# Turns as products on diagonal tiles, and key products that alternate between two row halves

## The chip, the cores and the metric

The kernel runs on one core of one Trainium2 chip. A core has TensorE (PE: matrix products, with a sequencer for loading weights, PEld), VectorE (DVE), ScalarE (ACT), GpSimd (POOL) and a queue for transfers (SP). The metric is the device time of one execution, in microseconds (us); lower is better. A time is the median of several runs.

## The reference, cut to what matters

A decoder trunk of four layers over 512 tokens of width 1024, in float32. Every layer is a mixer followed by a gated MLP with a short convolution. The mixers are sparse attention, mLSTM, the delta-rule mixer (RWKV-7), and sparse attention again. The change is in the delta-rule mixer, of which there is one. It has 16 heads of width 64:

```python
def step(state, inp):
    r_t, w_t, k_t, v_t, kk_t, a_t = inp
    removed = jnp.einsum('bhij,bhj->bhi', state, kk_t)
    state = (state * w_t[:, :, None, :] - removed[..., None] * (kk_t * a_t)[:, :, None, :]
             + v_t[..., None] * k_t[:, :, None, :])
    return state, jnp.einsum('bhij,bhj->bhi', state, r_t)

_, y = lax.scan(step, jnp.zeros((B, H, N, N), f32), (tm(r), tm(decay), tm(k), tm(v), tm(kk), tm(a)))
...
y = ((y - mean) * lax.rsqrt(var + RWKV_GN_EPS)).reshape(B, T, D) * ln_w + ln_b
```

Projections come before this recurrence, a group norm, a gate and an output projection behind it.

## The kernel before, in words

The whole trunk is one program. Features lie on the 128 partitions, tokens along the row, so the mixer holds its 16 heads as 8 pairs: the first head of a pair on partitions 0 to 63 (`hv[0]`), the second on 64 to 127 (`hv[1]`). The 512 tokens are 8 chunks of 64.

The recurrence is computed by chunks. For each pair of heads six stages run one after the other: `prep` (decays and scaled operands), `inverse` (products within a chunk, the keys turned, the first levels of a triangular inverse), `last` (the other levels, and `inverted`), two halves of `scan` (the state from chunk to chunk), and `output` (group norm, gate). A loop of 13 steps starts a new pair at each step, so up to six pairs are under way, each at another stage.

Two helpers matter here.

`turn` transposes a 64x64 block of one head by means of PE and the identity. A block that ends on the lower partitions is a transpose instruction (L1664), one that ends on the upper partitions a product with the identity (L1666). It is called for both heads of a pair one after the other: 4 times in `inverse`, 4 times in `inverted`, and twice 8 times in `output` (once for the values that `scan` left, tile `sv`, and once for the normed output, tile `tmp`). That is 24 turns of both heads for each pair of heads. A turn's weights and operand lie on one head's 64 partitions, its result on 64 partitions of PSUM, so it uses one quarter of the PE array. For the values the result lies on the other head's partitions, so these two quarters are the ones off the diagonal.

The key products (L1761) multiply 64 rows of `KB` (keys of both kinds, 128 columns) with two blocks of `LW`. They use 64 rows and all columns of the array: the row half of their head. For each pair of heads there are 16, four for each head and half of the chunks, and each four fill one PSUM bank (`iv`), which three VectorE instructions then read.

Other small products of the loop: L1752 (64x64 products of both heads on the two diagonal tiles), L1775 (keys transposed, 128x128), L1804, L1812, L1819 (levels of the inverse), L1847, L1849, L1861, L1868 (the scan), L1876 (its output).

The order on every engine isn't the order in which the code is written. `Order` takes the traced program, gives each instruction a cost and each dependency a latency, makes list schedules forwards and backwards in turn for each phase, and keeps the best; the whole mixer is one phase. For PE it knows three things that matter here: a transpose counts 2 passes and an f32 product 4; the clock is taken to be half if too few columns went through the array in the tick before (`TICK`, `WARM`); and a product whose output is at most 64 rows and lies on the upper half is taken to run beside the one before it, if that was on the lower half and less than `BESIDE` ago (fields `alone`, and `lower` in `run`).

Of the kernel before, what the change touches and what calls it, by code (L numbers as in the profile page):

```python
# [26 lines left out]
# the FFN's blocks by Winograd's seven products instead of eight, and where its down projection goes on to the next chunks  # L27
# [4 lines left out]
def interleave(live):  # L32
    """advance generators [gen, done, expected] so that they finish together"""
    live = list(live)
    while live:
        it = min(live, key=lambda v: v[1] / v[2])
        try:
            next(it[0])
            it[1] += 1
        except StopIteration:  # L40
            live.remove(it)
# [11 lines left out]
BESIDE = 22  # L53

class Order:
    """a static order for every engine: list schedules of the traced program, forwards and backwards in turn"""

    def __init__(self, traced):
        ins = [i for i in traced if type(i).__name__.startswith("Inst")]  # L60
        self.ins, n = ins, len(ins)
        self.pred = [dict() for _ in ins]      # name -> latency after the end
        self.follow = [set() for _ in ins]     # starts after the start of
        self.eng, self.dur, self.table, self.rows, self.load, self.alone = [], [], [], [], [], []
# [9 lines left out]
        for k, i in enumerate(ins):  # L74
# [5 lines left out]
            # columns through the whole of the array  # L80
            self.rows.append(math.prod(x[1] for x in list(i.outs[0].bass_ap.ap)) * list(i.ins[0].bass_ap.ap)[0][1]
                             * self.passes(i) / 16384 if e == "PE" else 0)
            # weights load beside the product before, if that is long enough;
            # a product on the upper half of the array runs beside the one before on the lower
            self.load.append(0.0)
            self.alone.append(None)
            if e == "PE":
                p, rows = self.box(i.outs[0])[7:]
                wide = i.ins[0].dtype in (mybir.dt.float32, F32R) and not i.is_transpose
                self.load[k] = rows * (1 + wide) / 2.4  # L90
                if rows <= 64:
                    self.alone[k] = self.dur[k] if p else 0
                    if p:
                        self.dur[k] = BESIDE
# [23 lines left out]
        # a slot is free again when the tile whose users end first has been used  # L118
# [15 lines left out]
        # the memory of a pool is free for the next when all its users are through  # L134
# [10 lines left out]
        # phases: each opens its pools when those of the one before are closed  # L145
# [37 lines left out]
    def box(a):  # L183
        """(tile, in PSUM, partitions, columns, tile object); a PSUM bank is held whole, by readers too"""
# [62 lines left out]
    def run(self, prio, back=False, origin=0.0):  # L247
# [11 lines left out]
        table, short, lower = None, 0, False  # L259
        ticks = collections.defaultdict(float)  # columns that left the array  # L260
        for _ in range(n):
# [19 lines left out]
            if e == "PE" and not back:  # L281
# [5 lines left out]
                if self.alone[k] and not (lower and t - free[e] < BESIDE):  # L287
                    d += self.alone[k] - dur[k]
                    short = self.alone[k]
                else:  # L290
                    short = dur[k]
                lower = self.alone[k] == 0
# [26 lines left out]
    def part(self, a, b):  # L319
        """the instructions from a to b by themselves"""  # L320
        p = object.__new__(Order)
        for name in ("ins", "eng", "dur", "table", "rows", "load", "alone"):
            setattr(p, name, getattr(self, name)[a:b])
# [6 lines left out]
    def turns(self, prio, rounds, origin=0.0):  # L330
        """the best of the schedules forwards and backwards in turn"""
# [10 lines left out]
    def best(self, tries=24, rounds=10, keep=4, log=None):  # L342
        """phase by phase: schedules of the phase by itself, the best of them tried behind the phases before"""
# [34 lines left out]
class Core:  # L378
# [33 lines left out]
    def spill(self, i, src):  # L412
        """the residual leaves the chip"""
# [11 lines left out]
    def psum(self, **banks):  # L425
        """shares the banks out to the uses of a phase"""
# [20 lines left out]
    def weights(self, ap, pool=False, raw=None, parts=None, pieces=1):  # L447
        """a unit's high and low parts"""
# [83 lines left out]
    def combos(self, g, ap):  # L532
        """Winograd's sums of the quarters of h (chunks k | k + 4, token halves): [B11 - B12 | B22 + that],
        [B12 - B22 | B21 - the second], in two parts each"""
# [26 lines left out]
    def ffn(self, ly, gcur, gnext, nsplit=True):  # L561
        nc, tc, A = self.nc, self.tc, self.A
        H = T // 2
        with ExitStack() as es:
# [15 lines left out]
            def gate(b, G):  # L580
                """convolution and silu"""
# [28 lines left out]
            def mm(ps, w, k0, rhs, start, stop):  # L610
                """four chunks of a quarter product"""
# [7 lines left out]
            def seven(b):  # L619
                """gate and value of block b by Winograd's seven products: rows (gate, value), chunk halves, token halves"""  # L620
# [58 lines left out]
            def down_part(p, o):  # L679
                """a part's share of output o, with the shares of the parts before"""  # L680
# [61 lines left out]
    def fm_steps(self, units, xhi, xlo, out, m=128, tag="ps", every=2, pool=False):  # L742
        """fm_block in pieces; appends the bank to out"""
# [13 lines left out]
    def stack_block(self, unit, xhi, xlo, m, dst, room, tag="ps"):  # L757
        """narrow product: both weight parts side by side, two passes; dst = sum of the halves"""
# [19 lines left out]
    def nsa(self, j, gnext):  # L778
        nc, tc, A = self.nc, self.tc, self.A
        te, ve, ac, po = nc.tensor, nc.vector, nc.scalar, nc.gpsimd  # L780
        with ExitStack() as es:
# [16 lines left out]
            # token-major values, high and low parts side by side  # L798
# [97 lines left out]
            with ExitStack() as cs:  # L896
# [36 lines left out]
                # gates  # L933
# [4 lines left out]
                # compression  # L938
                raws = [fp.tile([128, 1024], F32, name="cw1", tag="cw1", bufs=3) for _ in range(8)]
                for i in range(2):  # L940
# [7 lines left out]
                    for k in range(16):  # L948
                        if (i, k) == (1, 0):
                            next(val)  # L950
                        if k % 4 == 0:
                            # the values' place is still free
# [42 lines left out]
            def cmp_soft(g):  # L995
# [23 lines left out]
                # block-diagonal compressed values of this group  # L1019
# [27 lines left out]
            def first_block():  # L1047
                # of the output, as far as the heads are through
# [9 lines left out]
            def scores(i):  # L1058
# [4 lines left out]
                for qbs in ((0, 1), (2,), (3,)):  # L1063
                    bank = self.ps(tag="s")
                    pss = []
                    # the masks of the diagonal blocks first, and what follows is added
# [116 lines left out]
    def mlstm(self, j, gnext):  # L1183
# [3 lines left out]
        with ExitStack() as es:  # L1187
# [30 lines left out]
            # gates  # L1218
# [182 lines left out]
            # per-head scale, tokens on partitions  # L1401
# [33 lines left out]
    def rwkv(self, j, gcur, gnext):  # L1435
# [4 lines left out]
        with ExitStack() as es:  # L1440
# [6 lines left out]
            # halves for the tanh forms of the sigmoids  # L1447
# [31 lines left out]
            # room that the second half of the values takes later  # L1479
# [6 lines left out]
            # the residual leaves the chip for this part, its place is taken by the normed input  # L1486
# [8 lines left out]
            def narrow(unit, n):  # L1495
                # the step from the token before follows the product, with weights scaled for it beside the plain ones
# [27 lines left out]
            for i in range(DC):  # L1524
                po.memset(Hn[i][:, 7:8], 0.0)
                ve.scalar_tensor_tensor(Hn[i][:, 8:], self.x[i], gcur[:, i:i + 1], self.R, op0=OP.mult, op1=OP.mult)
                # the step from the token before, kept where the values come later
# [33 lines left out]
            # kept where the groups' operands come later  # L1561
# [14 lines left out]
            # normaliser of the removal keys  # L1576
# [37 lines left out]
            def values(c):  # L1614
                # tokens of a chunk on the half that the other head's state leaves free
# [37 lines left out]
            def block_diagonal(p):  # L1653
                # operands that are zero beside their blocks
# [5 lines left out]
            def turn(out, src, e, low):  # L1660
                # a transpose that ends on the upper partitions is a product with the identity
                eye = self.ident[hv[e], hv[e]]
                if low:
                    te.transpose(out, src, eye)  # L1664
                else:
                    te.matmul(out, src, eye, start=True, stop=True)  # L1666
# [9 lines left out]
            def prep(p):  # L1676
# [38 lines left out]
                # bonus coefficients on every feature of the head  # L1715
# [7 lines left out]
                # scaled operands; first head of the pair holds (-b|k), second (k|-b)  # L1723
# [16 lines left out]
            def inverse(p):  # L1740
                g = G[p]
                KB, LW = g["KB"], g["LW"]
                # in-chunk products
# [11 lines left out]
                for e in range(2):  # L1755
                    kr, br = hv[1 - e], hv[e]
                    for q in range(2):
                        ps = self.ps((128, 4, 2, 64), tag="iv")
                        for i in range(4):
                            c = 4 * q + i  # L1760
                            te.matmul(ps[:, i], KB[br, c], LW[br, e:e + 2, c], start=True, stop=True)  # L1761
                        cs4 = slice(4 * q, 4 * q + 4)
# [6 lines left out]
                # keys with tokens on partitions  # L1769
# [411 lines left out]
```

## Time and profile before

| | us |
|---|---|
| three runs | 3009.51, 3031.78, 3043.8 |
| their median | 3031.78 |
| profiled execution, span of the core | 3045.1 |
| mean granted PE clock in it | 0.943 |

The profiled execution is one execution besides the three; its span, from the first to the last instruction, is the time that the rows of the trace add up to, and it lies 13 us above the median of the runs. In the views, PE rows with f32 products count two records for each product. Matmuls are pipelined, so durations of neighbours overlap: what a run of products costs is read from its start to the start of what comes next. The granted clock is given as a share of full speed.

### The profile page before, as it was taken

Reading aid. Unit: us, or ns where it says so; the run is one execution under the profiler, and the core shown is the slowest. Engines: PE = TensorE matmul, PEld = TensorE weight load, DVE = VectorE, ACT = ScalarE, POOL = GpSimd, SP = SyncE. Lnnn points to the kernel's source line nnn. Section 1 sums busy time; section 2 is a strip of 40 time slices with the busy share of each in tenths; the row PEclk is TensorE's granted clock in tenths of the full one; section 3 lists DMA queues with packets and bytes.
Section 4 is the critical chain, followed back from the end, with each engine's and each line's share of the span. In section 5 each row is a group of like instructions: output and inputs, shape, how many; then the busy total and the mean of one; then the engine's idle time right before and its main releaser. Section 6 shows DMA issues by size and latency. Waiting matters only on the chain. (4 is left out here: it accounts for less than half of the span.)

```text
span 3045.1 us, 48538 instructions
## 1 busy us (share of the span) xinstructions
PE 2936.2 (96%) x17768; PEld 2450.8 (80%) x17768; DVE 2357.0 (77%) x4225; ACT 1622.7 (53%) x3290; POOL 814.5 (27%) x898
## 2 busy tenths in 40 slices
PE   7999999999999999989899999999999999999998
PEld 6777899997777999867666666689997777889996
DVE  8688789988788898886565533499987788888995
ACT  4677655544665554435454433355543677755543
POOL 5476300001351000034664332200003467400001
PEclk8999999999999999999986656899999999999999
DMA  4100223454123334532100000223445210133344
GB/s 159 59 29 22 91 98 122 135 158 142 65 88 121 105 122 143 163 122 84 42 5 4 5 19 30 92 96 121 135 153 161 77 37 27 39 125 110 131 135 149
DMA packets 115422, 283.28 MB, mean 93 GB/s; under 512 B 14448, under 2 KB 26224, under 8 KB 115184
## 3 DMA queue, kind: packets, MB, share of 16 engines
q1 hardware_dynamic: 115184, 280.18, 28.0%
q8 instruction: 140, 2.29, 0.3%
q14 instruction: 98, 0.80, 0.1%
HBM read 248.67 MB, written 31.46 MB: 92 GB/s over the span
## 5 line engine op out<-in xcount | busy, mean ns | idle before, releaser
L461 ACT ACTIVATE whi<-wraw 128x1024 fp32r<-128x1024 f32 (+2 forms) x344 | 272.3, 792 | 453.9 <-PE ps L469 292.0
L616 PE MATMUL ps<-h,shi 128*128 128x256 f32 x1728 | 353.7, 281 | 0.0
L462 DVE TENSOR_TENSOR wlo<-wraw,whi 128x512 fp32r<-128x512 f32 (+2 forms) x306 | 275.8, 902 | 81.8 <-ACT whi L461 78.7
L616 PE MATMUL ps<-bhi,slo 128*128 128x256 f32 x1152 | 322.9, 281 | 0.1
L616 PE MATMUL ps<-blo,shi 128*128 128x256 f32 x1152 | 321.9, 281 | 0.0
L616 PE MATMUL ps<-bhi,shi 128*128 128x256 f32 x1152 | 321.9, 281 | 0.0
L601 POOL MEMSET tmp<- 128x2 f32 x88 | 8.3, 100 | 1097.9 <-DVE tmp L594 873.8
L616 PEld LDWEIGHTS ps<-h,shi 128*128 128x128 f32 x1728 | 282.8, 188 | 7.4
L469 PE MATMUL ps<-alo,whi 128*128 128x512 f32 x704 | 278.3, 396 | 0.0
L468 PE MATMUL ps<-ahi,wlo 128*128 128x512 f32 x704 | 277.0, 394 | 0.0
L467 PE MATMUL ps<-ahi,whi 128*128 128x512 f32 x704 | 276.8, 395 | 0.0
L467 PE MATMUL ps<-h,whi 128*128 128x512 f32 x672 | 265.2, 399 | 4.8 <-ACT whi L461 1.4
L468 PE MATMUL ps<-h,wlo 128*128 128x512 f32 x672 | 263.8, 394 | 1.8 <-DVE wlo L462 1.5
L469 PE MATMUL ps<-h,whi 128*128 128x512 f32 x672 | 263.7, 394 | 0.0
L616 PE MATMUL ps<-h,slo 128*128 128x256 f32 x864 | 242.6, 281 | 0.0
L734 DVE TENSOR_TENSOR slo<-sum,shi 128x512 fp32r<-128x512 f32 x288 | 197.3, 686 | 44.8 <-ACT shi L733 43.0
L733 ACT ACTIVATE shi<-sum 128x512 fp32r<-128x512 f32 x288 | 179.4, 624 | 94.6 <-DVE sum L636 67.1
L616 PEld LDWEIGHTS ps<-bhi,slo 128*128 128x128 f32 x1152 | 217.0, 188 | 5.5 <-DVE slo L734 0.5
L616 PEld LDWEIGHTS ps<-bhi,shi 128*128 128x128 f32 x1152 | 216.5, 188 | 4.3 <-ACT shi L733 0.2
L616 PEld LDWEIGHTS ps<-blo,shi 128*128 128x128 f32 x1152 | 216.5, 188 | 1.5
L501 POOL TENSOR_TENSOR tmp<-tmp 128x512 f32<-128x512 f32 x62 | 97.1, 1566 | 351.8 <-ACT tmp L496 347.3
L1089 POOL TENSOR_SCALAR P<-P,st,GT 128x128 f32<-128x128 f32 (+3 forms) x256 | 161.5, 646 | 86.3 <-DVE st L1087 53.6
(677 smaller groups left out, 7977.1 us busy)
## 6 DMA issues: line engine op xcount, KB each, us to landing
wraw<-in_fup_dram SPq DMA_DIRECT2D x104, 512.0 KB, 3.6
fraw<-in_fup_dram SPq DMA_DIRECT2D x72, 512.0 KB, 3.5
wraw<-in_fdn_dram SPq DMA_DIRECT2D x128, 256.0 KB, 2.8
share<-xt SPq DMA_DIRECT2D x64, 256.0 KB, 2.1
xt<-share SPq DMA_DIRECT2D x64, 256.0 KB, 3.0
wraw<-in_fdn_dram SPq DMA_DIRECT2D x64, 192.0 KB, 2.5
x<-spill SPq DMA_DIRECT2D x48, 256.0 KB, 3.1
spill<-x SPq DMA_DIRECT2D x47, 256.0 KB, 2.6
```

Source lines behind the costliest of these rows:

```text
L461: nc.scalar.activation(hi[:, s], raw[:, s], AF.Copy)
L462: (nc.gpsimd if pool else nc.vector).tensor_tensor(lo[:, s], raw[:, s], hi[:, s].bitcast(F32), op=OP.subtract)
L467: t.matmul(ps, whi, xhi, start=start, stop=False)
L468: t.matmul(ps, wlo, xhi, start=False, stop=False)
L469: t.matmul(ps, whi, xlo, start=False, stop=stop)
L501: nc.gpsimd.tensor_tensor(a2, self.acc[0], sq, op=OP.add)
L601: nc.gpsimd.memset(G[:, 0:2], 0.0)
L616: nc.tensor.matmul(ps, lhs[:, s], x, start=start and k + i == 0, stop=k == 3 and i == 2, skip_group_check=True)
L733: self.nc.scalar.activation(hi, src, AF.Copy)
L734: self.nc.vector.tensor_tensor(lo, src if src2 is None else src2, hi.bitcast(F32), op=OP.subtract)
L1089: po.tensor_scalar(P[qb], P[qb], st[:, 2, qb:qb + 1], GT[:, qb, 3 * h + 1 + br:3 * h + 2 + br], op0=OP.mult, op1=OP.mult)
```

## The change

It has three parts, all for the delta-rule mixer's small products.

1. `turn` always makes a product with the identity, for both heads. The transposes on the lower half (L1664) are gone; the line is L1670 now.
2. In `inverse`, the key products of one half of the chunks are written for both heads in turn, into two banks, chunk by chunk (L1765); before, all those of the first head came first, then those of the second. What reads the banks is unchanged but for its order.
3. `Order` now also takes a product that uses 64 rows and more than 64 columns of the array to run beside the one before it, if that was of the same kind and on the lower row half. A new field `side` tells the kinds apart: 1 for products with at most 64 output rows, as before, 2 for those with at most 64 operand rows.

Comments are removed as well. No tile, size or transfer is changed.

```diff
@@ Order.__init__
             if e == "PE":
                 p, rows = self.box(i.outs[0])[7:]
+                kind = 1
+                if rows > 64:
+                    b = self.box(i.ins[0])
+                    p, kind = b[2], 2
+                    if b[3] - b[2] > 64:
+                        kind = 0
                 wide = i.ins[0].dtype in (mybir.dt.float32, F32R) and not i.is_transpose
                 self.load[k] = rows * (1 + wide) / 2.4
-                if rows <= 64:
+                if kind:
+                    self.side[k] = kind
                     self.alone[k] = self.dur[k] if p else 0
                     if p:
                         self.dur[k] = BESIDE
@@ Order.run
-                if self.alone[k] and not (lower and t - free[e] < BESIDE):
+                if self.alone[k] and not (lower == self.side[k] and t - free[e] < BESIDE):
                     d += self.alone[k] - dur[k]
                     short = self.alone[k]
                 else:
                     short = dur[k]
-                lower = self.alone[k] == 0
+                lower = self.side[k] if self.alone[k] == 0 else 0
@@ Core.rwkv
-            def turn(out, src, e, low):
-                eye = self.ident[hv[e], hv[e]]
-                if low:
-                    te.transpose(out, src, eye)
-                else:
-                    te.matmul(out, src, eye, start=True, stop=True)
+            def turn(out, src, e):
+                te.matmul(out, src, self.ident[hv[e], hv[e]], start=True, stop=True)
...
-                for e in range(2):
-                    kr, br = hv[1 - e], hv[e]
-                    for q in range(2):
-                        ps = self.ps((128, 4, 2, 64), tag="iv")
-                        for i in range(4):
-                            c = 4 * q + i
-                            te.matmul(ps[:, i], KB[br, c], LW[br, e:e + 2, c], start=True, stop=True)
-                        cs4 = slice(4 * q, 4 * q + 4)
+                for q in range(2):
+                    pss = [self.ps((128, 4, 2, 64), tag="iv") for _ in range(2)]
+                    for i in range(4):
+                        c = 4 * q + i
+                        for e in range(2):
+                            te.matmul(pss[e][:, i], KB[hv[e], c], LW[hv[e], e:e + 2, c], start=True, stop=True)
+                    cs4 = slice(4 * q, 4 * q + 4)
+                    for e in range(2):
+                        kr, br = hv[1 - e], hv[e]
+                        ps = pss[e]
                         ve.tensor_tensor(MT[br, 2 * q:2 * q + 2], ps[br, 0::2, e],
                                          m_su[br, None, :].to_broadcast([64, 2, 64]), op=OP.mult)
...
-                        turn(pg[hv[e], d], F2[hv[e], d], e, e == 0)
+                        turn(pg[hv[e], d], F2[hv[e], d], e)
```

The other three calls of `turn` lose their last argument in the same way.

More of the change, by code (lines that the diff above doesn't have):

```diff
@@ L63, in __init__ @@
         self.follow = [set() for _ in ins]
-        self.eng, self.dur, self.table, self.rows, self.load, self.alone = [], [], [], [], [], []
+        self.eng, self.dur, self.table, self.rows, self.load, self.alone, self.side = [], [], [], [], [], [], []
         tiles, users, tags = {}, collections.defaultdict(list), collections.defaultdict(list)
@@ L86, in __init__ @@
             self.alone.append(None)
+            self.side.append(0)
             if e == "PE":
                 p, rows = self.box(i.outs[0])[7:]
+                kind = 1
[4 more added lines that the diff above has]
+                        kind = 0
                 wide = i.ins[0].dtype in (mybir.dt.float32, F32R) and not i.is_transpose
                 self.load[k] = rows * (1 + wide) / 2.4
-                if rows <= 64:
+                if kind:
+                    self.side[k] = kind
                     self.alone[k] = self.dur[k] if p else 0
@@ L258, in run @@
                 heapq.heappush(wait[eng[k]], (0.0, prio[k], k))
-        table, short, lower = None, 0, False
+        table, short, lower = None, 0, 0
         ticks = collections.defaultdict(float)
@@ L321, in part @@
         p = object.__new__(Order)
-        for name in ("ins", "eng", "dur", "table", "rows", "load", "alone"):
+        for name in ("ins", "eng", "dur", "table", "rows", "load", "alone", "side"):
             setattr(p, name, getattr(self, name)[a:b])
@@ L1830, in inverted @@
                     for e in range(2):
-                        turn(pg[hv[e], d], F[hv[e], d], e, e == 0)
+                        turn(pg[hv[e], d], F[hv[e], d], e)
                 g["XT"] = XT = pair(rk())
@@ L1901, in output @@
                     for e in range(2):
-                        turn(pt[hv[e], c], S[hv[1 - e], c, e, :], 1 - e, e == 0)
+                        turn(pt[hv[e], c], S[hv[1 - e], c, e, :], 1 - e)
                 ve.tensor_tensor(c8(bon), pt, c8(bon), op=OP.mult)
@@ L1907, in output @@
                     for e in range(2):
-                        turn(pt[hv[e], c], c8(yc)[hv[e], c], e, e == 0)
+                        turn(pt[hv[e], c], c8(yc)[hv[e], c], e)
                 ac.activation(yf, pt.rearrange("p c t -> p (c t)"), AF.Identity, scale=vec(LNW, p), bias=vec(LNB, p))
```

## The prediction

> **What bounds the kernel now.** I read the page's first two parts, then busy time by stretches, then PE's rows in order of time inside the delta-rule mixer.
>
> From the page: engines, then PE and its granted clock in 40 slices of 76 us.
>
> ```profile
> PE 2936.2 (96%) x17768; PEld 2450.8 (80%) x17768; DVE 2357.0 (77%) x4225; ACT 1622.7 (53%) x3290; POOL 814.5 (27%) x898
> ...
> PE   7999999999999999989899999999999999999998
> ...
> PEclk8999999999999999999986656899999999999999
> ```
>
> PE is busy nearly everywhere, and its clock is full but for slices 21 to 26: the mixer's loop over pairs of heads, which I take as 1500 to 1960 us.
>
> The view by stretches (us, then busy time of PE, PEld, DVE, ACT, POOL, granted clock, DMA):
>
> ```profile
> 1500.00:1684.00 184.00, 177.87 (x1395) 126.73 (x1393) 114.66 (x257) 95.61 (x278) 101.81 (x122) 0.80 0.02 4
> 1684.00:1960.00 276.00, 275.60 (x1799) 185.60 (x1796) 106.61 (x286) 99.53 (x320) 81.91 (x89) 0.65 0.09 28
> 1960.00:3045.10 1085.10, 1049.79 (x6467) 920.43 (x6465) 905.63 (x1643) 603.28 (x1169) 231.35 (x272) 0.99 0.33 108
> 1684.61:1688.02 3.41, 3.41 (x31) 2.35 (x30) 1.18 (x3) 0.68 (x4) 3.41 (x5) 1.00 0.00 0
> 1688.02:1691.43 3.41, 3.41 (x23) 2.48 (x22) 1.79 (x5) 1.51 (x6) 0.05 (x1) 0.50 0.09 24
> 1740.00:1760.00 20.00, 20.00 (x112) 12.16 (x112) 5.90 (x13) 5.63 (x18) 4.68 (x6) 0.50 0.01 4
> ```
>
> In the loop PE idles 6 of 460 us, while DVE, the next engine, is busy 221. The clock is 1.00 or 0.50, never between, in steps of 3.41 us; from 0.80 and 0.65 follows 184 x 0.40 + 276 x 0.70 = 267 us at half clock. So the loop costs what PE's products cost at the clock they get, and what PE saves is saved.
>
> **The turns.** PE in order of time: start, duration, operation. Durations overlap, so I go from start to start. First half clock, then full, then runs of L1752, which has what a turn has after the change: 64x64 products of both heads on two diagonal tiles, into one bank. A product in f32 is two records.
>
> ```profile
> 1640.53 0.31 PE L1664 MATMUL a<-ident,sv 64*64 64x64 f32 x1
> 1640.77 0.47 PE L1666 MATMUL a<-ident,sv 64*64 64x64 f32 x2
> 1641.17 0.31 PE L1664 MATMUL a<-ident,sv 64*64 64x64 f32 x1
> ...
> 1571.01 0.24 PE L1664 MATMUL iv<-ident,h 64*64 64x64 f32 x1
> 1571.18 0.33 PE L1666 MATMUL iv<-ident,h 64*64 64x64 f32 x2
> 1571.44 0.24 PE L1664 MATMUL iv<-ident,h 64*64 64x64 f32 x1
> ...
> 1586.99 0.68 PE L1752 MATMUL iv<-wraw,LW 64*64 64x64 f32 x16
> 1587.60 0.33 PE L1868 MATMUL sa<-sv,wlo 128*64 128x64 f32 x2
> ...
> 1776.89 1.11 PE L1752 MATMUL iv<-wraw,LW 64*64 64x64 f32 x14
> 1777.93 0.58 PE L1761 MATMUL iv<-LW,wraw 64*128 64x128 f32 x1
> ```
>
> A pair of turns (transpose for one head, product for the other) takes 0.64 us at half clock and 0.43 at full. Diagonal products take 0.61 us for four pairs at full clock, 0.15 a pair; 1.04 for three and a half at half clock, 0.30 a pair; entering and leaving the run is in it.
>
> ```profile
> L1664 PE MATMUL a<-ident,sv x64: 242/310/313, 1638.0 to 1943.0; 64*64 64x64 f32 x64
> L1664 PE MATMUL a<-ident,tmp x64: 241/309/314, 1646.8 to 1956.7; 64*64 64x64 f32 x64
> L1664 PE MATMUL iv<-ident,h x56: 213/243/311, 1532.1 to 1876.1; 64*64 64x64 f32 x56
> L1664 PE MATMUL iv<-ident,x x8: 215/242/244, 1503.0 to 1543.6; 64*64 64x64 f32 x8
> ```
>
> There are 64 + 64 + 56 + 8 = 192 pairs. The medians lie at the half-clock duration for two groups (310) and at the full one for the others (243), so I put 96 at each: 96 x 0.64 + 96 x 0.43 = 103 us before, 96 x 0.30 + 96 x 0.15 = 43 after. At the same clock this saves 60 us, on PE, which waits for nothing there. The order shows that such runs are really built. PE, output of the first pair of heads, the end of a stretch in which L1664 and L1666 take turns: before,
>
> ```order
> L1775 MATMUL iv<-ident,wraw 128x128 x3
> L1664 MATMUL a<-ident,sv_14814 64x64
> L1666 MATMUL a<-ident,sv_14814 64x64
> L1775 MATMUL iv<-ident,wraw 128x128
> L1868 MATMUL sb<-sv_14814,wlo 64x64 x2
> ```
>
> and now (lines are 4 to 8 higher; L1782 is the old L1775, L1854, L1856 and L1868 the scan's products):
>
> ```order
> L1670 MATMUL a<-ident,sv_14814 64x64 x7
> L1868 MATMUL sa<-up,rk 64x64 x2
> L1670 MATMUL a<-ident,sv_14814 64x64 x3
> L1854 MATMUL sb<-sv_14814,LW 64x64 x2
> L1856 MATMUL sb<-sv_14814,LW 64x64 x2
> L1670 MATMUL a<-ident,sv_14814 64x64 x6
> L1782 MATMUL iv<-ident,wraw 128x128 x4
> ```
>
> The single transposes and products became runs of one form. A third of the turns, those of the values (sv), sit on the two off-diagonal tiles, of which no row shows a run; I price them alike.
>
> The Trainium skill ("TensorEngine Tiling (Array Packing)", Gotcha 1: PSUM Pressure) says that different row tiles cannot access one PSUM bank at the same time, and both heads' turns go into one bank. The L1752 run above writes one bank from both row halves at 0.15 us a pair, so the trace speaks against the rule here.
>
> **The key products.** 16 a pair of heads, 128 in all. L1761 at half clock, at full clock, and at the one later place where two products of one head are followed at once by two of the other:
>
> ```profile
> 1560.42 2.07 PE L1761 MATMUL iv<-LW,wraw 64*128 64x128 f32 x8
> 1562.42 0.48 PE L1819 MATMUL iv<-h 128*64 128x128 f32 x2
> ...
> 1522.78 1.16 PE L1761 MATMUL iv<-LW,wraw 64*128 64x128 f32 x8
> 1523.86 0.50 PE L1682 MATMUL a<-hid,ws 128*128 128x512 f32 x1
> ...
> 1628.27 1.23 PE L1761 MATMUL iv<-LW,wraw 64*128 64x128 f32 x8
> 1629.43 0.49 PE L1819 MATMUL iv<-h 128*64 128x128 f32 x2
> ```
>
> Four products take 2.00 us, or 1.08 at full clock; across the two heads 1.16 instead of 2.00. With every pair so, half of them at each clock, 16 x 0.84 + 16 x 0.45 = 21 us would go. But the planner does not keep the alternation. PE, keys of the fifth pair of heads, before (iv_17403 is the first head's bank, iv_17449 the second's):
>
> ```order
> L1761 MATMUL iv_17403<-LW_17128,wraw_17129 128x128 x2
> L1861 MATMUL sb_17501<-up_17462,rk_16867 64x64 x2
> L1761 MATMUL iv_17403<-LW_17128,wraw_17129 128x128 x2
> L1761 MATMUL iv_17449<-LW_17128,wraw_17129 128x128 x2
> L1819 MATMUL iv_17443<-h_16315,h_17345 64x128
> ```
>
> and now (iv_17449 first head, iv_17450 second):
>
> ```order
> L1765 MATMUL iv_17449<-LW_17128,wraw_17129 128x128
> L1868 MATMUL sb_17501<-up_17467,rk_16867 64x64 x2
> L1765 MATMUL iv_17449<-LW_17128,wraw_17129 128x128 x3
> L1854 MATMUL sa_17473<-sv_14814,LW_16444 64x64 x2
> L1856 MATMUL sa_17473<-sv_14814,LW_16444 64x64 x2
> L1765 MATMUL iv_17450<-LW_17128,wraw_17129 128x128 x4
> ```
>
> One head's four come first, then other work, then the other's. Of 64 neighbours only the four of the first pair of heads' second half alternate, and two other places adjoin. I take 1 us, between 0 and 4; the 21 us do not come.
>
> **The clock.** Turns per 3.41 us step (only L1664's rows counted), first and last of the 13 steps in the loop after which the clock fell, and the two with four pairs after which it didn't:
>
> ```profile
> 1531.01:1534.42 3.41, 0.97 (x4) 0.42 (x4) 1.00 0.00 0
> ...
> 1954.26:1957.67 3.41, 1.53 (x7) 0.65 (x6) 1.00 0.00 0
> 1667.54:1670.95 3.41, 0.97 (x4) 0.42 (x4) 1.00 0.01 2
> 1916.71:1920.13 3.42, 0.97 (x4) 0.42 (x4) 1.00 0.44 135
> ```
>
> Every one of the 13 falls follows a step with at least four pairs of turns; no step at full clock with fewer was followed by a fall. PE was as busy there as elsewhere (3.41 of 3.41 us above, then 0.50): it is the thinness of the work. Eight pairs of turns at full clock fill a whole step today (8 x 0.43); after the change they fill 1.2 us of it and the rest holds denser products. So most falls should go.
>
> Bounds: if all stay, the gain is the 60 us. If none stays, the 267 - 61 = 206 us of half clock that aren't turns shrink by the ratio of the key rows, 2.00 / 1.08, to about 112; with 193 - 41 = 152 us at full clock and 192 x 0.15 + 6 = 35 of turns (6 for runs under four pairs) the loop takes 299, a gain of 161. DVE's 221 us fit, but not loosely: from 1500 to 1684 its 115 us would stand against about 137 of PE (74 at half clock, of which 13 are turns, become 33; 110 less 14 of turns at full; 8 of turns), 84%. I take a fifth of the loop at half clock instead of 58%, since waits will thin out some steps: 299 / (0.8 + 0.2 / 1.85) = 329, and 14 us of PE waiting for DVE, ACT and POOL in the first part: 343. The gain is 117, and 1 for the keys.
>
> Beside the loop: PE's order ahead of the mixer is the same row for row; behind the loop the planner has reordered the same instructions. PE idles 35 of 1085 us there; I take nothing, and 12 us either way for the range. The counts of instructions and DMAs are unchanged on every engine.
>
> Sum: 3045.1 - 118 = 2927 for a profiled execution. The median of the runs is 3031.8, 0.9956 of the profiled span, so 2915.
>
> **Rivals.**
> (A) The clock's share stays. For it: half-clock steps hold other thin work (1740 to 1760 is at 0.50 with PE busy 20.00). Against it: 13 of 13. Gain 61: 2984, as a median 2971. The Trainium skill ("TensorE: Matmul & The Clock Gate", Part 1) has the gate follow how busy PE is; by that rule, with PE already busy throughout, this case would hold. The step at 1684.61, fully busy and then at 0.50, disagrees.
> (B) Both heads' turns run one after the other in the one bank: a steady pair, 0.12 at full and 0.21 at half clock (the runs above less their ends), comes on top: 96 x 0.12 + 96 x 0.21 = 32 us of the 60 go. 3045 - 28 = 3017, median 3004.
> (C) Slower: a turn that is its own product pays the switch of tiles at both ends, as a lone product does:
>
> ```profile
> 1560.02 0.47 PE L1861 MATMUL sa<-up,rk 64*64 64x64 f32 x2
> ...
> 1588.23 0.33 PE L1861 MATMUL sb<-up,rk 64*64 64x64 f32 x2
> 1588.48 0.27 PE L1868 MATMUL sa<-sv,wlo 128*64 128x64 f32 x1
> ```
>
> 0.40 us at half clock (to 1560.42), 0.25 at full. Two such make 0.80 and 0.50: 96 x 1.30 = 125 against 103, or 192 x 0.80 = 154 if turns then hold the clock down. 22 to 51 us slower, a median of 3054 to 3083; it decides above 0.64 and 0.43 a pair. Against it: the L1752 rows.
> (D) No fall is left and DVE keeps up: 3045 - 162 = 2883, median 2870.
>
> **The numbers.** Forecast 0.62, A 0.20, B 0.06, C 0.04, D 0.08. The forecast's own range is 2885 to 2950 (a tenth to two fifths of half clock). The range reaches to A with its 12 us, 2985, and to D, 2870; B and C and the edges are left out. About 1% is what a measurement tells from no change here, since the three runs span 1.1%: faster by more takes the forecast, A, D and a little of B, 0.91; within 1% most of B and some of C, 0.05; slower 0.04.
>
> **What would show it.** Right: L1670 in runs at about 0.15 and 0.30 us a pair; a clock of 0.85 or more from 1500 to 1850; few falls after turns; L1765 still at 2.00 and 1.08 us for four. Wrong: L1670 at 0.25 or more a pair at full clock (B, C); a clock near 0.70 in the loop (A); PE idle over 40 us in the loop, which would mean that DVE or a chain of waits took over; or the stages behind the loop off by more than 12 us.

## The result, and the profile after

The changed kernel takes 2907.89 us (median of four runs, 2905.01 to 2914.75) against 3033.13 for the kernel before beside it (3009.51 to 3043.8): a ratio of 0.9614, 95% interval 0.9579 to 0.9649. The forecast was 2915. The profiled execution spans 2904.2 us, 141 less than that of before; the sum had 118.

The page of the changed kernel: engines, then PE and its granted clock in 40 slices of 73 us.

```profile
PE 2789.4 (96%) x17960; PEld 2357.7 (81%) x17960; DVE 2363.3 (81%) x4225; ACT 1622.5 (56%) x3290; POOL 820.8 (28%) x898
...
PE   7999999999989999998899999999998999999998
...
PEclk9999999999999999999989999999999999999999
```

The trough of the clock is gone; one slice at 8 is left. PE's 17,960 records are 192 more than before: each transpose became a product, which has two.

The view by stretches of the changed kernel (us, then busy time of PE, PEld, DVE, ACT, POOL, granted clock, DMA). The second row is the loop (1500 to 1960 before), the third what comes behind it:

```profile
1500.00:1684.00 184.00, 172.78 (x1769) 122.75 (x1768) 143.78 (x314) 111.78 (x336) 116.26 (x139) 0.91 0.02 6
1500.00:1819.00 319.00, 305.43 (x3336) 218.51 (x3335) 222.91 (x537) 188.69 (x591) 179.70 (x205) 0.95 0.08 27
1819.00:2904.20 1085.20, 1049.37 (x6467) 919.71 (x6465) 907.14 (x1642) 605.27 (x1169) 236.04 (x272) 0.99 0.33 108
```

The loop went from 460 to 319 us, and that is the whole 141: behind it stand 1085.2 us against 1085.1. PE waits 14 us in the loop, 11 of them in its first part.

PE's rows of the changed kernel in order of time: turns on the diagonal, turns of the values (off the diagonal), four keys at full clock, four at half.

```profile
1533.02 0.68 PE L1670 MATMUL iv<-ident,h 64*64 64x64 f32 x16
1533.64 0.55 PE L1826 MATMUL iv<-h 128*64 128x128 f32 x6
...
1653.84 0.68 PE L1670 MATMUL a<-ident,sv 64*64 64x64 f32 x16
1654.46 0.66 PE L1782 MATMUL iv<-ident,wraw 128*128 128x128 f32 x4
...
1582.24 1.16 PE L1765 MATMUL iv<-LW,wraw 64*128 64x128 f32 x8
1583.33 0.33 PE L1854 MATMUL sa<-sv,LW 128*64 128x64 f32 x2
...
1517.15 2.07 PE L1765 MATMUL iv<-LW,wraw 64*128 64x128 f32 x8
1519.15 1.12 PE L1819 MATMUL iv<-h 128*64 128x128 f32 x8
```

Four pairs of turns take 0.62 us from start to start, on the diagonal and off it. Four keys take 1.09 and 2.00 us, as before.

For the comparisons below I went through PE's rows from the first turn to the last, from each start to the next start, and put the time to turns, keys or other products; time in which no PE record runs is idle. The last column is how long the clock was at half. All in us:

```
kernel                          length  turns  keys  other  idle | half clock
before                           453.9  101.0  47.8  298.9   6.2 | 266.2
keys only                        429.7   93.8  43.7  281.8  10.5 | 204.8
before, other seed               435.8   99.3  39.9  288.8   7.8 | 218.5
changed kernel                   318.7   32.1  36.1  236.9  13.6 |  34.1
changed kernel, again            314.1   32.1  33.3  233.8  14.9 |  20.5
changed kernel, other seed       318.0   34.2  35.6  231.9  16.3 |  27.3
turns only                       325.3   36.5  33.6  234.4  20.7 |  27.3
output's turns only              328.8   51.1  28.8  233.6  15.3 |  37.5
alternation kept                 327.0   36.2  25.8  242.5  22.5 |  41.0
turns in before's order          306.6   29.6  32.7  233.3  10.9 |   6.8
turns in before's order, again   307.2   29.8  32.7  233.4  11.3 |   6.8
turns head by head               338.6   49.8  31.4  238.8  18.6 |  51.2
alternation, old turn cost       299.3   30.4  22.2  228.6  18.1 |   3.4
```

### The profile page after: what moved, and what is told of

Its sections match the earlier page's. It is cut to its first block, busy times and chain, and to the rows that moved or that the text cites. A ratio compares the mean times of both kernels' runs of the same rounds, so it can differ in the third digit from the quotient of the medians.

```text
span 2904.2 us, 48935 instructions
## 1 busy us (share of the span) xinstructions
PE 2789.4 (96%) x17960; PEld 2357.7 (81%) x17960; DVE 2363.3 (81%) x4225; ACT 1622.5 (56%) x3290; POOL 820.8 (28%) x898
## 5 line engine op out<-in xcount | busy, mean ns | idle before, releaser
L475 PE MATMUL ps<-h,whi 128*128 128x512 f32 x672 | 266.0, 398 | 4.0 <-ACT whi L469 1.2
L1097 POOL TENSOR_SCALAR P<-P,st,GT 128x384 f32<-128x384 f32 (+3 forms) x256 | 161.8, 646 | 81.8 <-DVE st L1095 52.0
```

The source lines that it names most:

```text
L475: t.matmul(ps, whi, xhi, start=start, stop=False)
L1097: po.tensor_scalar(P[qb], P[qb], st[:, 2, qb:qb + 1], GT[:, qb, 3 * h + 1 + br:3 * h + 2 + br], op0=OP.mult, op1=OP.mult)
```

## The experiments

My theory was that the turns bring the gain, half as cheaper work and half through the clock, which falls after steps with four or more mixed pairs of turns; and that the key part does nothing, because the planner undoes it. Against it stood three others: that the key part or its planner rule carries something; that it isn't the number of mixed pairs that the clock follows, but how much passes through the array in a step; and that the gain comes from a new plan, since the planner counts a transpose with 2 passes and a product with 4, so that every order moves.

### The two parts apart

The kernel before with its turns as products, keys and planner as they were:

```diff
             def turn(out, src, e, low):
-                eye = self.ident[hv[e], hv[e]]
-                if low:
-                    te.transpose(out, src, eye)
-                else:
-                    te.matmul(out, src, eye, start=True, stop=True)
+                te.matmul(out, src, self.ident[hv[e], hv[e]], start=True, stop=True)
```

> Only the turns of the change; key products and planner as before. Theory T (the turns carry all of the gain, by overlapping and by no longer pulling the clock down; the keys give 1 us): 2909 us, within 12, granted clock in the mixer's loop at 0.93 or more, loop about 320 us long. Rival K (the keys and the planner's new rule carry a part, up to the 21 us that were worked out for full alternation): 2920 to 2930 us.

Measured: 2919.23 us, ratio 0.9634 (0.9601 to 0.9666). The turns alone bring nearly everything, within the 12 us of Theory T but only 1 us short of Rival K's range, so this run does not yet exclude K. The 11 us to the changed kernel are no price of the keys yet: the orders of the two kernels differ throughout, and a mere change of the planner's seed moves about as much (9 us, below).

The changed kernel with before's mixed turns, so that only the key part and the planner's rule are left:

```diff
-            def turn(out, src, e):
-                te.matmul(out, src, self.ident[hv[e], hv[e]], start=True, stop=True)
+            def turn(out, src, e, low):
+                eye = self.ident[hv[e], hv[e]]
+                if low:
+                    te.transpose(out, src, eye)
+                else:
+                    te.matmul(out, src, eye, start=True, stop=True)
...
-                        turn(pg[hv[e], d], F2[hv[e], d], e)
+                        turn(pg[hv[e], d], F2[hv[e], d], e, e == 0)
```

(and the other three calls of `turn` likewise).

> Only the key products and the planner's new rule; turns are still a transpose and a product. Theory T: 3032 us, within 12 of before, granted clock in the loop about 0.71 as before, with falls after steps that hold four or more mixed turns. Rival K: 3012 us or less.

Measured: 3024.47 us, ratio 0.9992 (0.9963 to 1.0021): nothing. Its loop, in the view by stretches:

```profile
1500.40:1930.10 429.70, 419.25 (x3162) 288.94 (x3162) 217.34 (x533) 190.02 (x590) 176.32 (x205) 0.76 0.06 20
```

The clock is still low, 0.76. That this loop is 24 us shorter than before's is no gain of the keys: the profiled execution (3018.3 us) lies at the low end of this kernel's runs (3019.97 to 3037.32) and that of before (3045.1) at the high end of its own.

### The planner's luck

Both kernels with another seed of the planner's random numbers (`random.Random(2)` for `random.Random(1)`).

> The change, with another seed for the planner's random tries: the same instructions in another order. How much of the time is the plan's luck: within 15 us of 2908 by all theories; what differs from it says how large a difference between two plans has to be before it tells anything.

> The kernel before with the same other seed. Within 20 us of 3033 by all theories, with a granted clock in the loop between 0.65 and 0.80; if a luckier plan could keep the clock up with the old turns too, as the run with mixed turns in the inverse did, the time falls below 2990.

Measured: the changed kernel 2916.63 us, ratio 0.9639 (0.9595 to 0.9683), 9 us above itself; the kernel before 3031.94, ratio 1.0025 (0.9992 to 1.0058). The 125 us are no accident of a plan, while differences of 10 us between these kernels may be.

### The same order, row for row

The kernel before with its turns as products, as in the first experiment, but with the planner told to count a turn that ends on the lower partitions as the transpose it was. With that the order of every engine is that of before, row for row; only the instruction differs.

```diff
+    def turned(i):
+        if i.is_transpose:
+            return True
+        if not any(Order.on_chip(a) and Order.box(a)[0].startswith("ident") for a in i.ins):
+            return False
+        return Order.box(i.outs[0])[7:] == (0, 64) and list(i.ins[0].bass_ap.ap)[0][1] == 64
...
-        return 2 if i.is_transpose else 4 if i.ins[0].dtype == mybir.dt.float32 else 1
+        return 2 if Order.turned(i) else 4 if i.ins[0].dtype == mybir.dt.float32 else 1
```

(and `turned` stands for `is_transpose` in two more lines of the planner).

> The kernel before with the turns as products on both halves, and the planner told to go on counting a lower turn as a transpose: every engine's order is that of before, row for row, and only what PE does for 192 turns differs. Theory T (the gain is made on PE by the products themselves: overlap, and more columns in each step of the clock gate): 2920 to 2945 us, granted clock in the loop at 0.9 or more. Rival R (a good part comes from the planner's new order, which the cheaper turns allow): 2960 us or more. Rival A of the prediction (overlap alone, the clock as before): 2970 us.

Measured: 2899.22 us, ratio 0.9585 (0.9539 to 0.9631). The gain does not come from a new plan; it is even 21 us larger than Theory T's range allowed. Before's loop from first to last turn, in the view by stretches:

```profile
1503.00:1956.90 453.90, 447.72 (x3169) 308.34 (x3170) 218.64 (x536) 193.54 (x595) 180.41 (x206) 0.71 0.06 19
```

and the same row of this kernel:

```profile
1499.90:1806.40 306.50, 295.59 (x3360) 212.43 (x3362) 222.90 (x536) 190.76 (x595) 183.34 (x206) 0.99 0.09 28
```

In one and the same order the clock goes from 0.71 to 0.99, and the page has no slice below 9:

```profile
PEclk9999999999999999999999999999999999999999
```

The split says what that is worth. The loop loses 147 us: 71 on turns, 15 on keys, 66 on other products, and PE idles 5 more. Keys and other products are the same instructions in the same order, so their 81 us should be the clock. The rows bear that out: if each line's products cost what the same line costs at full clock in before, keys and others together would take 266.0 us, and they take 266.0 (346.7 in before). Of the turns' 71, 192 x 0.43 = 83 us would be their full-clock price mixed, so 101 - 83 = 18 are the clock too, and 83 - 30 = 53 the cheaper pair. About 99 of the 147 us came by way of the clock, which the edit doesn't touch in so many words.

### What the clock follows

The changed kernel with the turns of `inverse` and `inverted`, a third of all, mixed again; the output's turns stay products.

```diff
-            def turn(out, src, e):
-                te.matmul(out, src, self.ident[hv[e], hv[e]], start=True, stop=True)
+            def turn(out, src, e, low=False):
+                eye = self.ident[hv[e], hv[e]]
+                if low:
+                    te.transpose(out, src, eye)
+                else:
+                    te.matmul(out, src, eye, start=True, stop=True)
...
-                        turn(pg[hv[e], d], F2[hv[e], d], e)
+                        turn(pg[hv[e], d], F2[hv[e], d], e, e == 0)
...
-                        turn(pg[hv[e], d], F[hv[e], d], e)
+                        turn(pg[hv[e], d], F[hv[e], d], e, e == 0)
```

> The change, but the turns in the inverse (64 of the 192 pairs, in runs of four) are a transpose and a product as before; only the 128 pairs in the output, in runs of eight, are products on both halves. Theory T (a step at full clock that holds four mixed pairs ends in a fall): the 8 falls that followed runs of four stay, the clock in the loop is between 0.75 and 0.85, and the time 2950 to 2985 us. Rival L (only the long runs matter, four mixed pairs among dense work are borne): the clock holds at 0.9 or more, and only 64 x (0.43 - 0.15) = 18 us are lost against the change: 2926 us. Rival P (the gain goes by pairs): 2908 + 125 / 3 = 2950 us.

Measured: 2925.14 us, ratio 0.9658 (0.9613 to 0.9702). This kernel has 13 steps at full clock with four mixed pairs, and in 10 of them the clock held. The view by stretches, of L1671 alone (its transposes: PE, PEld, clock, DMA), and then of everything in two of these steps and the step behind each:

```profile
1643.39:1646.80 3.41, 0.97 (x4) 0.42 (x4) 1.00 0.01 2
1622.91:1626.32 3.41, 0.94 (x4) 0.43 (x4) 1.00 0.07 20
...
1643.39:1646.80 3.41, 3.41 (x52) 2.67 (x49) 2.83 (x8) 3.18 (x8) 1.42 (x3) 1.00 0.01 2
1646.80:1650.22 3.42, 3.42 (x46) 2.76 (x46) 2.94 (x10) 1.42 (x7) 1.80 (x3) 1.00 0.02 5
1622.91:1626.32 3.41, 2.57 (x29) 1.76 (x28) 3.29 (x8) 2.22 (x12) 2.05 (x2) 1.00 0.07 20
1626.32:1629.73 3.41, 3.41 (x28) 2.28 (x28) 1.31 (x3) 1.22 (x5) 2.28 (x4) 0.50 0.02 4
```

Both have four mixed pairs. The first has 52 PE records and no gap, and the clock stays at 1.00; the second has 29 and a gap of 0.84 us, and 0.50 follows. The three steps that fell idled 0.54 to 0.93 us, those that held at most 0.27. So "four mixed pairs and the clock falls" is wrong, and Rival L's time and clock (2926 us, 0.94 in the loop) are the ones that came. In before, such pairs came in steps with little else in them, and I took the company for the cause.

The kernel with the key part only, whose turns are all mixed, says the same where PE never idles: of its 18 steps at full clock with four or more mixed pairs, 8 held. One that held, with six pairs, and one that fell, with five, each with the step behind it:

```profile
1794.50:1797.91 3.41, 3.41 (x42) 2.58 (x40) 0.00 (x0) 2.92 (x12) 0.00 (x0) 1.00 0.48 154
1797.91:1801.33 3.42, 3.42 (x31) 2.28 (x31) 0.48 (x2) 1.87 (x6) 1.48 (x3) 1.00 0.00 0
1756.95:1760.36 3.41, 3.41 (x29) 2.15 (x29) 0.14 (x1) 1.38 (x6) 1.33 (x2) 1.00 0.17 68
1760.36:1763.78 3.42, 3.42 (x22) 2.28 (x22) 1.55 (x3) 0.34 (x3) 1.72 (x2) 0.50 0.01 2
```

PE is busy throughout both; what differs is how much passes through it, 42 records against 29.

What does better: for each step I added up the columns that went through PE, each weighted with the share of the array that it used, four passes for an f32 product and two for a transpose. By this count a mixed pair is 64 + 32 = 96 in 0.43 us, 762 in a step filled with them; two products are 128 in 0.15 us, 2910. The old turns drew a step below before's dividing line, the new ones don't.

It is no law yet. The two steps above had 2112 and 1696, but the clean parting is before's alone: with the key part only, falls go up to 2368 and four of the 54 steps that held lie below 2560; in before with another seed, falls go up to 2944 and again four of 54 that held lie below 2560, the lowest at 1856. In this experiment three steps with 1920 to 2304 and four mixed pairs held, PE idling at most 0.21 us in them; in the changed kernel's loop three steps with 2336 to 2496 held, and its three falls came after steps with 2944, 2688 and 1728. In the view by stretches:

```profile
1504.42:1507.83 3.41, 1.86 (x9) 0.98 (x8) 3.29 (x7) 1.39 (x5) 1.60 (x2) 1.00 0.00 0
1562.45:1565.86 3.41, 2.19 (x33) 1.44 (x30) 3.15 (x6) 2.82 (x10) 3.41 (x3) 1.00 0.00 0
1593.17:1596.58 3.41, 1.95 (x22) 1.25 (x21) 3.36 (x4) 3.02 (x11) 3.25 (x3) 1.00 0.00 0
```

There PE waits 1.2 to 1.6 us in a step in which DVE is busy nearly throughout. Idling alone doesn't decide either: the step at 1835.51 of the same kernel idles 1.83 us, with a count of 3072, and the clock held. How thin work and waiting add up is open.

That transposes are not needed for a fall is seen in before with the other seed. This step holds none at all, only f32 products, PE never idles in it, its count is 2688, and the clock fell behind it:

```profile
1676.27:1679.68 3.41, 3.41 (x34) 2.54 (x30) 2.34 (x7) 3.16 (x10) 1.20 (x2) 1.00 0.00 0
1679.68:1683.10 3.42, 3.42 (x16) 2.42 (x15) 1.95 (x7) 2.40 (x6) 2.07 (x3) 0.50 0.00 0
```

Such falls are rare: among steps at full clock with no mixed pair and PE idle under 0.1 us, this and one with 2304 (alternation kept) are the only falls below 2950, and 67 such steps of all kernels held, down to 2176. How much of a mixed pair's effect is its thinness and how much the transpose itself stays open.

### What the overlap of the two heads is worth

The changed kernel, but in each group all turns of one head come first, then all of the other, and the planner is held to it.

```diff
+                if kind == 1 and any(self.on_chip(v) and self.box(v)[0].startswith("ident") for v in i.ins):
+                    if turns and turns[0] == self.box(i.outs[0])[0]:
+                        self.follow[k].add(turns[1])
+                    turns = (self.box(i.outs[0])[0], k)
...
-                for d in range(4):
-                    for e in range(2):
+                for e in range(2):
+                    for d in range(4):
                         turn(pg[hv[e], d], F2[hv[e], d], e)
```

(and the three other loops around `turn` likewise).

> The change, but in each group of turns all products of the first head come before all of the second, and the planner is held to that: 279 of 384 follow a product on the same tile, so they don't overlap. Theory T: a product alone takes 0.117 us at full clock, a pair 0.23 instead of 0.12 and with 64 columns for 0.117 us too thin for the gate where a run is long: 192 x 0.117 = 22 us more, and a few falls: 2925 to 2960 us. Rival S (getting rid of the switch between transpose and product is the gain, overlap is not needed because PE waits for others): 2908 to 2915 us.

Measured: 2933.56 us, ratio 0.9691 (0.9634 to 0.9748). Without alternation the turns cost 49.8 us, 0.26 a pair, against 32.1; the whole is 26 us slower than the changed kernel, and still 97 faster than before (3030.33 beside it). That is Theory T's range; Rival S's 2915 us and less did not come. Most of the gain does not need the two heads in alternation, only that no transposes stand in between. Even here the heads are not wholly apart. PE in order of time, four turns of one head and then four of the other:

```profile
1536.27 0.93 PE L1675 MATMUL iv<-ident,h 64*64 64x64 f32 x16 [0.34 <-DVE h L1794]
1537.13 0.66 PE L1831 MATMUL iv<-h 128*64 128x128 f32 x8
```

0.86 us, where eight products one behind the other, at the 0.12 us of the steady pair in the prediction's (B), would take 0.94 and the two ends.

### The alternation of the keys, really built

The changed kernel, with the planner forced to keep the keys of the two heads in turn:

```diff
+                if kind == 2 and self.box(i.outs[0])[0].startswith("iv"):
+                    if keys and keys[0] % 8:
+                        self.follow[k].add(keys[1])
+                    keys = (keys[0] + 1 if keys else 1, k)
```

> The change, and the planner is held to the written order of the key products, so that the two heads' products do alternate (85 of 128 have one of the other row half just before them). Theory T (two row halves overlap, 4 products take 0.56 us at full clock where they took 1.08, and PE is what the loop waits for): up to 64 pairs x 0.22 = 14 us less than the change, 2894 us. Rival W (with the clock full, DVE, ACT and the waits between the stages set the loop's length as much as PE): 2908 us within 5, PE idle longer in the loop.

Measured: 2918.18 us, ratio 0.9628 (0.9596 to 0.966). PE in order of time, eight keys of both heads:

```profile
1646.15 1.16 PE L1770 MATMUL iv<-LW,wraw 64*128 64x128 f32 x16
1647.24 0.34 PE L1859 MATMUL sa<-sv,LW 128*64 128x64 f32 x4
```

Eight take 1.09 us, as long as four did. The effect that the change is after exists, at its full size: the keys fall from 36.1 to 25.8 us. But PE's idle time rises from 13.6 to 22.5, and other products by 5.6 at a clock that is no better; the loop is 8 us longer. Two banks must now be free at the same time before the eight can start, and the three VectorE instructions behind each head come together; which of these makes the wait was not tried apart. Neither expectation was met: the time is 5 us beyond Rival W's, whose reason (PE idles longer) is seen, and 10 us above the changed kernel, about what another seed moves, so a loss by the alternation itself is not shown.

### The old turn cost and the alternation together

Two of the planner's edits in one kernel: the alternation kept (the "fourth run" of the texts below), and a lower turn counted as a transpose (the "fifth run", the one in before's order). Beside it, on the same chip, once more the kernel in before's order and the changed kernel.

> The change with the key products held to alternate, as in the fourth run, and the planner told to count a lower turn as a transpose, as in the fifth. If the fifth run was fast because the old turn cost makes plans that suit the chip better, and alternation is worth its 10 us of PE: 2885 to 2895 us. If alternation is eaten by waits here too: 2899 us or more, with PE idle over 18 us in the loop. If the fifth run's plan was luck: 2905 to 2920 us.

> The fifth run's kernel again, beside the change on one chip: 2895 to 2905 us; the change beside it 2905 to 2912 us.

> The change itself, beside the two others on one chip: 2905 to 2912 us. If it comes out within 4 us of the fifth run's kernel, the difference between the new plan and the old is nothing that can be told.

Measured: both edits 2895.88 us, ratio 0.9575 (0.9538 to 0.9611); before's order again 2897.25, ratio 0.9579 (0.9542 to 0.9616); the changed kernel again 2907.85, ratio 0.9611 (0.9568 to 0.9655). The loops of the first two in the view by stretches, first to last turn, the first kernel

```profile
1503.50:1802.80 299.30, 281.24 (x3357) 199.87 (x3356) 219.95 (x536) 189.74 (x594) 185.07 (x207) 0.99 0.09 29
```

and the second:

```profile
1502.30:1809.50 307.20, 295.83 (x3361) 212.63 (x3362) 223.59 (x536) 191.03 (x595) 183.02 (x206) 0.99 0.09 28
```

The alternation takes 14.6 us of PE's busy time (295.8 to 281.2) and shortens the loop by 8, with PE idle 18 us in it; of the whole 1.4 us are left. In these two executions the loop starts 1.2 us later and what stands behind it takes 3.5 us longer. The time falls between the two expected ranges (up to 2895, from 2899), so whether the alternation is worth anything is not told; it isn't worth building here. But before's order with the new turns beats the change: its runs (2894.84 to 2901.1) and those of the changed kernel (2906.44 to 2912.81) don't meet, some 10 us or 0.4%; of the four runs of before's order in the experiment above, one (2907.52) does lie among them. The split names where: 6.8 us at half clock against 34.1 in the one execution of the changed kernel and 20.5 in the other. At 1 - 1.09 / 2.00 = 0.46 us lost for each, that is 12.6 and 6.3 us; the loops differ by 12 and 7. That a plan made with the dearer turn should let the clock fall less often is seen in two such plans (2896 to 2899 us) and four without it that also have all turns as products in alternation (2908 to 2919); why, no run tells.

## Why the prediction was right, point by point

**The price of the turns: right.** 0.15 us a pair at full clock was forecast from L1752 and came out as 0.62 for four, off the diagonal as on it. All turns: 101 us before against 103 worked out, 32 after against 35 at full clock. No turn of the changed kernel ran at half clock; with the turns only, 90 records did, at 0.29 a pair against the 0.30 forecast.

**The keys: right, for the reason given.** Alone they bring 0.9992. What the prediction didn't have: even where they alternate, the time doesn't follow. The 21 us were a figure at half and full clock mixed; the 10 us that were left at the better clock were lost again in the one plan that has them, 9 of them as waits of PE.

**The clock: right in direction, too cautious, and reasoned from the wrong mark.** The forecast left a fifth of the loop at half clock, 0.2 x 329 = 66 us; measured were 34 (20 to 51 in the six executions with all turns as products and planned with their true cost, 3 to 7 in the three planned with the old one). The 32 us too many are worth 32 x 0.46 = 15 of the 24 us by which the loop came out shorter than 343; nearly all the rest lies in the base of 299 (319 less 14 of waiting and 34 x 0.46 = 16 of half clock is 289; the 112 in the base should have been 111). The inference "13 of 13 falls follow four mixed pairs" fell with the kernels in which only the output's turns are products, or none. It gave the right sign, since it was the mixed pairs that kept before's steps thin, but as a rule it would have called this experiment's 10 holding steps wrong.

**PE's waits: right.** 14 us forecast for the first part, 11 measured there and 14 in the whole loop. These waits, not the turns, now stand ahead of the falls.

**Behind the loop: right.** 1085.2 against 1085.1, with 12 us allowed either way.

**The sum.** 2927 forecast for a profiled execution and 2904.2 measured, 23 us apart; the medians are only 7 apart (2915, 2907.89). The factor 0.9956 hid the rest: before's profiled execution stood 13 us above its median, the changed kernel's 4 below. Before's runs scatter by 1.1%, the changed kernel's by 0.3%, so the factor was a matter of that one execution and not of the kernel. That the forecast came within 7 us and not 23 is luck in this factor.

**The rivals.** (A), the clock's share stays: excluded by the same order at 0.71 and 0.99. The Trainium skill ("TensorE: Matmul & The Clock Gate", Part 1) has the gate follow how busy PE is; PE's busy share fell in that comparison, from 447.72 of 453.9 us to 295.59 of 306.5, and the clock rose, so busy time as the profile counts it is not the measure. Part 4 of that page says that transposes do not count as PE work for the gate in the way products do. The exchange of transposes for products agrees in sign; but with all transposes counted as nothing, L1775 and L1804 too, before's falls would lie at up to 2240 and its holding steps from 1536, counted with two passes they part at 2432 and 2560. Only one holding step makes that difference (the next lies at 2432), so it is a hint and no proof; the fall behind a step without any transpose, shown above, says that transposes are not the whole of it.

(B), one behind the other in the one bank: 0.15 us a pair says no, and the kernel that does run them head by head needs 0.26. (C), a lone product's price at every turn: 0.50 us a pair at full clock is excluded, 32.1 us for 192 pairs are 0.17. (D), no fall is left: not in the change, but nearly in before's order with the new turns, whose 2897 to 2899 us are its neighbourhood and not its 2870; at that clock PE idles 11 us and its products take 296.

## What to carry to other kernels

Where PE is always busy and its granted clock still low, count what passes through the array in a step, columns by share of the array, before counting instructions: replacing the thinnest ones can speed up everything beside them. A regularity such as "each fall follows this instruction" wants the counterexample looked for, the same instruction in a dense step, before it is taken for a cause. And when an edit changes what a planner believes, run it once in the old order too: here the old order was the better one, and only that comparison could show what the edit itself did.

## What was not expected of the hardware

- **The clock goes with what passes through the array, not with how long PE is busy.** In one order, with less busy time, half clock went from 266 to 7 us; in before's loop a weighted count near 2500 columns a step parts falls from holds. Other orders of the mixed turns keep to it only roughly, and steps in which PE also waits do not.
- **Products of the second row half start before all earlier ones of the first are through.** Four turns of one head and then four of the other take 0.86 us, and two keys and two keys 1.16 instead of 2.00 in the row that the prediction shows, where the order is first, first, second, second. Alternation in the order is not needed for every overlap.
- **The runs' scatter goes with the clock.** It was 1.1% before and 0.3% after. In the 13 runs of before beside the first experiment, the fastest, 3003.94 us, was granted 0.961 and the slowest, 3047.67, 0.944. That is 2 x 0.017 x 3030 = 103 us more at half clock; at 0.46 lost for each, 47 us, where the two are 44 apart. A loop near full clock is no guarantee: the kernel with the output's turns only scatters by 0.8%, from 2917.93 us at 0.983 to 2941.62 at 0.971.
